# Linear attention: state updates dealt one sample at a time, and two loads of the small tokens' weights moved into the gate stage

## The chip, the cores and the metric

The kernel runs on one core of one Trainium2 chip. The metric is the device time of one launch in microseconds. The engines are named as in the profile: PE multiplies matrices, PEld loads its weights, DVE (VectorE), ACT (ScalarE) and POOL (GpSimd) work elementwise, and SP only issues DMAs. SPq is SP's queue: it issues in order, so a DMA that waits for a semaphore holds back those behind it.

## The reference, cut to what matters

One inference step of a two-layer trunk. A prompt of 1,024 tokens goes through gated linear attention (4 heads, key width 128, value width 256, 1024 channels), an MLP, differential attention and another MLP. Beside it go the **small tokens**: 16 meta tokens in front of the prompt and one new token of each of 8 running sequences, the samples. A sample's attention state (4 heads of 128 x 256) is read, used and written back updated:

```python
def gla_chunk(state, q, k, v, lg):
    ...
    o_inter = jnp.einsum('blhd,bhde->blhe', q * jnp.exp(b), state)
    ...
    new_state = jnp.exp(b_last)[..., None] * state + jnp.einsum(
        'blhd,blhe->bhde', k * jnp.exp(b_last[:, None] - b), v)
    return new_state, o_inter + o_intra
```

For a sample the chunk is a single token, so the new state is the old one scaled per key channel, plus the outer product of its key and its value. The small tokens then pass the rest of layer 0 (output projection, post-norm, MLP, post-norm) and the input projection of layer 1, all in the first sixth of the kernel.

## The kernel before, in words

The kernel is written in program order, and a planner lays down each engine's queue ahead of the run: it walks a modelled timeline, takes what is ready there, and the earlier line first where several are. So moving a line changes its rank among what the model holds ready, and not directly its place in the queue. On the chip each queue then runs in the order laid down, with semaphore waits.

All that the change touches lies in the first 500 us, the linear attention. Matmuls of the prompt are done in three passes of split operands (`mm3`, L206 to L208). The stages in program order are:

- Head 0's projections and decays; meanwhile the small tokens' input projection (L530, L539).
- The small tokens' own attention (L541 to L673). `state_in` (L638) loads a sample's state into one of five buffers: three in `Y`, columns 5120 to 8191, two in `st2`. L645 multiplies them with the queries into the bank `po`.
- `small_tokens` (L752) is a generator for the small tokens' way through the rest. A step is one pair of weight loads (`swt`, two buffers of 1 MB, loaded by `sload`, L234, or `sload2`, L240) and, at the next step, 16 matmuls of the pair (L685 or L696). There are 24 pairs: 2 of the attention's output weights, 8 and 8 of the MLP's, 4 and 2 of layer 1's input projection. Between them lie two post-norms (`s_post`, `s_ln`, L699 to L740: a copy out of the bank by DVE, four transposes, some fifteen small operations on DVE, and a logarithm and an exponential on ACT). The last step writes key and value rows and `sxd` to memory (L784 to L790).
- `state_updates` (L647): per sample a broadcast load of its value row into one of two halves of `Y`, columns 4096 to 6143 (L654), a multiply with the key by POOL (L655, 128x1024), four multiply-adds on DVE (L657, 128x256) and the store of the state (L658). Three samples' states are loaded a second time (L652). The second half of the value buffer overlaps the first state buffer, and the first half holds the samples' values `sv`, which L631 reads. In the kernel before all eight come in one go within step 3 of `small_tokens`, behind the first post-norm.
- Heads 1 to 3 (L798): eight groups of projections each (`proj`: four groups of query and key, four of value; `proj` yields after each, evictions L313, L315, L391), then for each half of the prompt `decays` (DVE and ACT, L435) and `advance` (L494), a serial chain.
- The gate stage (L812): for each head and half, 48 matmuls of the gate r, SiLU on ACT (L825), transposes, and L833 on DVE. Its results go into `Y`, which becomes the input of the output projection (`w_out`, L1001) after L997.

`deal` makes one step of `small_tokens`. In the kernel before it is called once ahead of head 1, then in each head behind groups 2, 4, 6 and 8 and behind both `decays`, and at the end of each half in the gate stage:

```python
for h in range(1, GH):
    for n, _ in enumerate(proj(h)):
        if n % 2:
            deal()
    ...
    for c in range(2):
        parts = decays(h, c, pgs[c])
        deal()
```

That makes 1 + 18 + 8 = 27 calls. The generator needs 25; the last two find it done. The second post-norm (call 19) falls to the second half of head 3, the last step (call 25) to the gate stage's third head.

Memory: buffers of the whole stage, `swt` among them, are given up at `p1.close()` (L836), behind the gate stage. The buffers of the paged attention, which starts there (L857 and on; pages by L877), are laid out after that.

Of the kernel before, what the change touches and what calls it, by code (L numbers as in the profile page):

```python
# [114 lines left out]
def hybrid_step(ctx, tc, A, dbg=None, upto=9):  # L115
# [4 lines left out]
    def bc(ap, shape, axis):  # L120
        return ap.unsqueeze(axis).broadcast_to(shape)
# [20 lines left out]
    def mmt():  # L142
        return banks["mm"].tile([P, 512], F32, name="mmt") if "mm" in banks else pairt()[:, 0]
# [4 lines left out]
    def smt():  # L148
        return banks["sm"].tile([P, 512], F32, name="smt")
# [48 lines left out]
    def kunit(w, c0):  # L198
        return unit(256, w.rearrange("(k p) n -> p k n", p=P)[:, :, c0 : c0 + 256])
# [5 lines left out]
    def mm3(ps, ah, al, bh, bl, first, last):  # L205
        TE.matmul(ps, ah, bh, start=first, stop=False)  # L206
        TE.matmul(ps, ah, bl, start=False, stop=False)  # L207
        return TE.matmul(ps, al, bh, start=False, stop=last)  # L208
# [13 lines left out]
    def s4():  # L222
        return spool.tile([P, 1024], F32, name="s4")

    def s2():
        return s2p.tile([P, 512], F32, name="s2")
# [33 lines left out]
    def qk_unit(h):  # L260
        return unit(P, *[wir[:, :, 512 * i + h * P : 512 * i + (h + 1) * P] for i in range(2)])
# [48 lines left out]
    def evict_qk(c, i, ps):  # L310
        t = g2.tile([P, 512], F32, name=("gq", "gk")[i])
        if i == 0:
            S.activation(t, ps, AF.Copy, scale=P ** -0.5)  # L313
        else:
            S.copy(t, ps)  # L315
        qk[c, i] = t
# [53 lines left out]
    def proj(h):  # L370
        hi, lo = qku if h == 0 else qk_unit(h)
        hv, lv = (w.rearrange("p (i k n) -> p i k n", i=2, n=P) for w in (hi, lo))
        for c in range(h == 0, 2):
            cs = slice(512 * c, 512 * c + 512)
            for i in range(2):
                ps = mmt()
                for k in range(NB):
                    mm3(ps, hv[:, i, k, :], lv[:, i, k, :], XH[:, k, cs], XL[:, k, cs], k == 0, k == NB - 1)
                evict_qk(c, i, ps)
                yield  # L380
        hi, lo = v0u if h == 0 else kunit(wi, 1024 + h * 256)
        hv, lv = (w.rearrange("p (k n) -> p k n", n=256) for w in (hi, lo))
        for c in range(2):
            for i2 in range(2):
                ps = mmt()
                for i in range(2):
                    t = 4 * c + 2 * i2 + i
                    for k in range(NB):
                        a = slice(t * P, (t + 1) * P)
                        mm3(ps[:, i * 256 : (i + 1) * 256], XH[:, k, a], XL[:, k, a], hv[:, k, :], lv[:, k, :], k == 0, k == NB - 1)  # L390
                S.copy(Yh[:, h, 4 * c + 2 * i2 : 4 * c + 2 * i2 + 2, :].rearrange("p i e -> p (i e)"), ps)  # L391
                yield
# [37 lines left out]
    def gate_in(h, c):  # L430
        pg = axt()
        TE.matmul(pg, wg[32 * c : 32 * c + 16, h * P : (h + 1) * P], gT[32 * c : 32 * c + 16, :], start=True, stop=True)
        return pg
# [159 lines left out]
    for hh in range(2):  # L593
        ps = smt()
        for i in range(2):
            h = 2 * hh + i
# [37 lines left out]
    def slot(i):  # L634
        t = Y[:, 5120 + 1024 * i : 6144 + 1024 * i] if i < 3 else st2[:, i - 3, :]
        return t.rearrange("p (h e) -> p h e", e=256)

    def state_in(b, i):  # L638
        with tc.issue_after(w_in):
            dma(slot(i), A["state_gla"][0, b].rearrange("h d e -> d h e"))  # L640
# [6 lines left out]
    def state_updates():  # L647

        for n, (b, i) in enumerate(((5, 0), (6, 1), (7, 2), (3, 3), (4, 4), (0, 3), (1, 4), (2, 3))):
            stt = slot(i)  # L650
            if b < 3:
                state_in(b, i)  # L652
            vb = Y[:, 4096 + 1024 * (n % 2) : 5120 + 1024 * (n % 2)].rearrange("p (h e) -> p h e", e=256)
            dma(vb.rearrange("p h e -> p (h e)"), A["vs"][b : b + 1, :].broadcast_to([P, D]))  # L654
            G.tensor_tensor(vb, vb, bc(skT[:, :, NM + b], [P, GH, 256], 2), op=ALU.mult)  # L655
            for h in range(GH):
                V.scalar_tensor_tensor(stt[:, h, :], stt[:, h, :], ses[:, h, b : b + 1], vb[:, h, :], ALU.mult, ALU.add)  # L657
            dma(A["gla_state_s"][0, b].rearrange("h d e -> d h e"), stt)  # L658

    so = spool.tile([P, 256], F32, name="so")  # L660
    ssq = spool.tile([P, 1], F32, name="ssq")
# [90 lines left out]
    def small_tokens():  # L752

        s_post((yield from s_rows(soT, A["gla_w_out"][0], NB)), 0, spool)
        state_updates()

        shT = s4().rearrange("p (k t) -> p k t", t=TS)
        for half in range(2):
            ps = yield from s_cols(sx, A["mlp_w1"][0], half * 2048)
            r = s2()  # L760
            S.activation(r, ps, AF.Relu)
            V.tensor_tensor(r, r, r, op=ALU.mult)
            pt = smt()
            for j in range(4):
                TE.transpose(pt[:, j * P : (j + 1) * P], r[:, j * P : (j + 1) * P], ident)
            V.tensor_copy(shT[:, 16 * half : 16 * half + 16, :].rearrange("p (c j) t -> p c j t", j=4),
                          pt.rearrange("p (j c t) -> p c j t", j=4, c=4))
        s_post((yield from s_rows(shT, A["mlp_w2"][0], 32)), 1, spool)

        pa = yield from s_cols(sx, wd, 0)  # L770
        sqkr = s2()
        S.copy(sqkr, pa)
        tmp = s2()[:, :128].rearrange("p (n d) -> p n d", d=16)
        rope(sqkr.rearrange("p (n d) -> p n d", d=64), pa.rearrange("p (n d) -> p n d", d=64), srope, 8, tmp)
        pb = yield from s_rows(sx, wd[:, 2048:3072], NB)
        svv = s2()
        S.copy(svv[64:, :], pb[64:, :])
        S.copy(svv[:64, :], svv[64:, :])
        V.tensor_tensor(svv[:64, :], svv[:64, :], pb[:64, :], op=ALU.add)
        for c in range(2):  # L780
            hs = slice(4 * c, 4 * c + 4)
            o = 64 + c * TS
            f = lambda ap: ap.rearrange("t h d -> t (h d)")
            dma(f(A["k_rows_p"][0, 0, 0:NM, hs, :]), sqkr[o : o + NM, :])  # L784
            dma(f(A["k_rows_s"][0, :, 0, hs, :]), sqkr[o + NM : o + NM + NS, :])
            dma(f(A["v_rows_p"][0, 0, 0:NM, hs, :]), svv[c * TS : c * TS + NM, :])
            dma(f(A["v_rows_s"][0, :, 0, hs, :]), svv[c * TS + NM : c * TS + NM + NS, :])
            dma(A["qs"][:, c * 512 : (c + 1) * 512], sqkr[c * TS + NM : c * TS + NM + NS, :])

        dma(A["sxd"], sx)  # L790

    small = small_tokens()

    def deal():
        next(small, None)

    deal()
    for h in range(1, GH):  # L798
        for n, _ in enumerate(proj(h)):
            if n % 2:  # L800
                deal()
        st = SM[:, h, :]
        pgs = [gate_in(h, c) for c in range(2)]
        for c in range(2):
            parts = decays(h, c, pgs[c])
            deal()
            st = advance(h, c, st, *parts)
        head_end(h, st)

# [2 lines left out]
    for h in range(GH):  # L812
        hi, lo = kunit(wi, 2048 + h * 256)
        hv, lv = (w.rearrange("p (k n) -> p k n", n=256) for w in (hi, lo))
        silt = st2.rearrange("p k (c n) -> p k c n", c=2)
        for c in range(2):
            cs = slice(512 * c, 512 * c + 512)
            sil, pts = [], []
            for m in range(2):
                ps = mmt()  # L820
                for k in range(NB):
                    ms = slice(m * P, (m + 1) * P)
                    mm3(ps, hv[:, k, ms], lv[:, k, ms], XH[:, k, cs], XL[:, k, cs], k == 0, k == NB - 1)
                s_ = silt[:, m, c, :]
                act = S.activation(s_, ps, AF.Silu).ins  # L825
                sil.append(s_)
                pt = axt()
                for i in range(4):
                    TE.transpose(pt[:, i * P : (i + 1) * P], Yh[:, h, 4 * c + i, m * P : (m + 1) * P], ident)
                pts.append(pt)  # L830
            deal()
            for m in range(2):
                V.scalar_tensor_tensor(fmv[:, h, c, m, :], pts[m], gn[:, m : m + 1], sil[m], ALU.mult, ALU.mult)  # L833
    with tc.issue_after(act):
        S.preload_act_table_set("natural_log_exp_and_others")
    p1.close()  # L836
# [548 lines left out]
    for step in steps + [None] * 0:  # L1385
        if step:
            h, n, t = step
# [356 lines left out]
```

## Time and profile before

| what | value |
|---|---|
| median of 3 runs | 2821.41 us (2813.26 to 2823.16) |
| the profiled execution | 2817.14 us |
| its span, first to last instruction | 2815.3 us |
| mean granted TensorE clock | 0.990 |
| PE busy | 2724.2 us (97%) |
| DVE, ACT, POOL busy | 1962.9, 1097.5, 1108.0 us |

The time of the profiled execution is 1.8 us over its span; what is shorter in the span is shorter in the time. PE is busy nearly throughout, so a change pays where PE stands idle or runs on a lower clock. Rows of the view by stretches give a stretch, its length, each engine's busy time with the number of its instructions, the granted clock, the DMA engines' busy share and the GB/s.

### The profile page before, as it was taken

How to read it: one execution, taken by the hardware profiler on the slowest of the kernel's cores; microseconds unless marked ns; L12 is line 12 of the kernel's file. 1: busy time of each engine (PE TensorE's matmuls, PEld its weight loads, DVE VectorE, ACT ScalarE, POOL GpSimd, SP SyncE). 2: the span in 40 equal slices, each digit the busy share in tenths (PEclk: the TensorE clock that was granted, in tenths of full speed). 3: DMA queues.
4: the chain of work that ended last, by engine and by line, in shares of the span. 5: the costliest groups of instructions: out<-in, count | busy, mean ns of one | idle time of the engine just before them, and what ended most of it. 6: DMA issues, size and time to landing. Idle time of an engine off the chain costs nothing.

```text
span 2815.3 us, 52242 instructions
## 1 busy us (share of the span) xinstructions
PE 2724.2 (97%) x19849; PEld 2238.2 (80%) x19849; DVE 1962.9 (70%) x3045; ACT 1097.5 (39%) x2232; POOL 1108.0 (39%) x744
## 2 busy tenths in 40 slices
PE   8988999999999999999999999899999999999997
PEld 5866766987777777777798989777898889798985
DVE  5365462578877787777568740887648888978788
ACT  4324363152221222222242112777525646355553
POOL 2142122334354343434233322200026767676774
PEclk9999999999999999999999999999999999999998
DMA  7565545735798898988658995212144555555684
GB/s 235 165 227 194 203 177 189 257 92 169 286 341 309 308 357 296 342 316 315 242 174 302 361 370 172 65 54 78 34 124 87 105 141 113 141 125 113 133 184 100
DMA packets 275624, 562.81 MB, mean 200 GB/s; under 512 B 23510, under 2 KB 144412, under 8 KB 271276
## 3 DMA queue, kind: packets, MB, share of 16 engines
q1 hardware_dynamic: 256076, 522.75, 53.9%
q0 software_dynamic: 19296, 36.71, 8.1%
q8 instruction: 156, 2.56, 0.4%
q14 instruction: 96, 0.79, 0.1%
HBM read 533.00 MB, written 29.52 MB: 200 GB/s over the span
## 4 chain that ended last, share of the span: by engine, by line
PE 78%; DVE 8%; DMA 5%; ACT 4%; issue 2%; POOL 2%; SPq 0%; DVEq 0%; POOLq 0%; ACTq 0%
PE mmt L206 18%; PE mmt L207 18%; PE mmt L208 18%; PE smt L949 4%; PE axt L206 3%; PE axt L207 3%; PE axt L208 3%; PE smt L1320 2%; ACT as L1298 1%; PE prt L1294 1%; DVE pg L908 1%; DMA swt<-in_mlp_w 1%; PE axt L1315 1%; POOL wlo L194 1%; DMA raw<-in_diff_w_in 1%
## 5 line engine op out<-in xcount | busy, mean ns | idle before, releaser
L194 POOL TENSOR_TENSOR wlo<-raw,whi 128x512 fp32r<-128x512 f32 x252 | 368.0, 1474 | 730.4 <-ACT whi L193 614.7
L206 PE MATMUL mmt<-whi,XH 128*128 128x256 f32 (+1 forms) x1760 | 524.3, 300 | 1.4 <-DVE ast L1296 0.9
L207 PE MATMUL mmt<-wlo,XH 128*128 128x256 f32 (+1 forms) x1760 | 522.1, 298 | 1.3 <-POOL wlo L194 1.3
L206 PE MATMUL mmt<-XH,whi 128*128 128x512 f32 (+1 forms) x1216 | 435.9, 360 | 7.1 <-DVE Y L1019 3.0
L208 PE MATMUL mmt<-XH,wlo 128*128 128x512 f32 (+1 forms) x1216 | 432.4, 356 | 0.0
L208 PE MATMUL mmt<-whi,XL 128*128 128x256 f32 x1536 | 431.7, 284 | 0.0
L193 ACT CAST whi<-raw 128x512 fp32r<-128x512 f32 x252 | 150.6, 619 | 572.9 <-DMA raw<-in_mlp_w 178.7
L206 PEld LDWEIGHTS mmt<-whi,XH 128*128 128x128 f32 x1760 | 330.4, 189 | 38.3 <-issue 25.1
L909 DVE TENSOR_REDUCE sc<-pg 128x16 f32<-128x1024 f32 x256 | 308.5, 1212 | 71.8 <-POOL pg L908 69.3
L207 PEld LDWEIGHTS mmt<-wlo,XH 128*128 128x128 f32 x1760 | 332.1, 189 | 18.5 <-issue 7.2
L207 PE MATMUL mmt<-XL,whi 128*128 128x512 f32 x768 | 306.9, 400 | 0.0
L908 DVE TENSOR_TENSOR pg<-pg,qb 128x1024 f32<-128x1024 f32 x192 | 258.9, 1355 | 66.6 <-DMA pg<-in_cache_k 49.7
L208 PEld LDWEIGHTS mmt<-whi,XL 128*128 128x128 f32 x1536 | 288.3, 189 | 4.8 <-issue 4.2
L206 PEld LDWEIGHTS mmt<-XH,whi 128*128 128x128 f32 x1216 | 229.8, 189 | 50.8 <-issue 7.9
L908 POOL TENSOR_TENSOR pg<-pg,qb 128x1024 f32<-128x1024 f32 x64 | 164.3, 2569 | 254.1 <-DMA pg<-in_cache_k 180.7
L208 PEld LDWEIGHTS mmt<-XH,wlo 128*128 128x128 f32 x1216 | 230.1, 189 | 36.3 <-issue 4.1
L206 PE MATMUL mmt<-whi,HH 128*128 128x512 f32 x512 | 205.3, 402 | 4.4 <-DVE Y L1133 4.4
L208 PE MATMUL mmt<-whi,HL 128*128 128x512 f32 x512 | 204.4, 399 | 0.0
L207 PE MATMUL mmt<-wlo,HH 128*128 128x512 f32 x512 | 203.9, 398 | 0.0
L1583 POOL TENSOR_TENSOR wlo<-RW,whi 128x512 fp32r<-128x512 f32 x96 | 167.0, 1771 | 66.3 <-ACT whi L1582 65.9
L1583 POOL TENSOR_TENSOR wlo<-rw,whi 128x512 fp32r<-128x512 f32 x92 | 155.6, 1768 | 78.3 <-ACT whi L1582 75.6
L207 PEld LDWEIGHTS mmt<-XL,whi 128*128 128x128 f32 x768 | 145.6, 190 | 37.4 <-issue 6.3
(438 smaller groups left out, 5729.2 us busy)
## 6 DMA issues: line engine op xcount, KB each, us to landing
pg<-in_cache_k SPq DMA_DIRECT2D x256, 512.0 KB
pg<-in_cache_v SPq DMA_DIRECT2D x256, 512.0 KB
raw<-in_mlp_w SPq DMA_DIRECT2D x164, 256.0 KB
swt<-in_mlp_w SPq DMA_DIRECT2D x32, 1024.0 KB
rw<-in_mlp_w SPq DMA_DIRECT2D x116, 256.0 KB
RW<-in_mlp_w POOLq DMA_DIRECT2D x96, 256.0 KB, 5.7
swt<-in_gla_w_in SPq DMA_DIRECT2D x12, 1024.0 KB
swt<-in_diff_w_in SPq DMA_DIRECT2D x12, 1024.0 KB
```

The costliest lines, as they stand in the source:

```text
L193: S.copy(hi[:, c], raw)
L194: G.tensor_tensor(lo[:, c], raw, hi[:, c].bitcast(F32), op=ALU.subtract)
L206: TE.matmul(ps, ah, bh, start=first, stop=False)
L207: TE.matmul(ps, ah, bl, start=False, stop=False)
L208: return TE.matmul(ps, al, bh, start=False, stop=last)
L908: eng.tensor_tensor(pg, pg, qb, op=ALU.mult)
L909: return V.tensor_reduce(sc[:, n, :], pg.rearrange("p (h d) -> p h d", d=64), op=ALU.add, axis=AX.X).ins
L949: m = TE.matmul(acc[i * TS : i * TS + 16, :256], w[r, n, :], pg[r, i * 256 : (i + 1) * 256], start=n == 0, stop=n == NPG).ins
L1294: TE.matmul(pss[m], qs[i][r, ts_], ks[j][r, x:y], start=i + j == 0, stop=i == 1)
L1298: S.activation(sc_[:, m, :W], sc_[:, m, :W], AF.Exp, bias=mns[:, m : m + 1], scale=-1.0, accum_out=l[:, m : m + 1])
L1320: TE.matmul(out, at, v, start=j == 0, stop=j == t + 1)
L1583: G.tensor_tensor(lo[:, k, :], t, hi[:, k, :].bitcast(F32), op=ALU.subtract)
```

## The change

- `state_updates` becomes a generator that yields after each sample. It is created beside `small_tokens`, and each of head 1's eight groups of projections is followed by one sample's update. So the updates no longer stand behind the first post-norm and ahead of the first pair of the MLP's weights; updates 1 to 3 come ahead of it, update 4 just ahead of its step, updates 5 to 8 behind it, between the next two pairs.
- In heads 2 and 3 the call of `deal` behind the first `decays` is dropped. That leaves 1 + 6 + 5 + 5 + 8 = 25 calls, so that two pairs more fall to the gate stage: the second post-norm goes to the gate stage's first head, second half, and the last step to its very end.
- Behind the gate stage a loop runs out what may be left of `small_tokens` (by this count nothing).

No arithmetic, load or store is added or dropped.

```diff
             dma(A["gla_state_s"][0, b].rearrange("h d e -> d h e"), stt)
+            yield
...
         s_post((yield from s_rows(soT, A["gla_w_out"][0], NB)), 0, spool)
-        state_updates()
-
...
-    small = small_tokens()
+    small, updates = small_tokens(), state_updates()
...
     deal()
     for h in range(1, GH):
         for n, _ in enumerate(proj(h)):
+            next(updates, None)
             if n % 2:
                 deal()
         st = SM[:, h, :]
         pgs = [gate_in(h, c) for c in range(2)]
         for c in range(2):
             parts = decays(h, c, pgs[c])
-            deal()
+            if c or h == 1:
+                deal()
             st = advance(h, c, st, *parts)
         head_end(h, st)
...
+    for _ in small:
+        pass
     with tc.issue_after(act):
         S.preload_act_table_set("natural_log_exp_and_others")
     p1.close()
```

## The prediction

> **What bounds the kernel now.** I read the page first: PE is the busiest engine by far.
>
> ```profile
> span 2815.3 us, 52242 instructions
> ...
> PE 2724.2 (97%) x19849; PEld 2238.2 (80%) x19849; DVE 1962.9 (70%) x3045; ACT 1097.5 (39%) x2232; POOL 1108.0 (39%) x744
> ```
>
> So 2815.3 - 2724.2 = 91.1 us is all that better order can win by filling PE's idle time. Next I read the view by stretches around the stages that the change touches, to see where those 91 us lie.
>
> ```profile
> 160.00:240.00 80.00, 65.33 (x632) 48.82 (x632) 60.96 (x113) 26.00 (x68) 33.69 (x16) 0.94 0.62 206
> ...
> 270.00:430.00 160.00, 151.57 (x1687) 108.88 (x1685) 92.18 (x198) 77.48 (x182) 31.97 (x19) 1.00 0.56 199
> 430.00:500.00 70.00, 69.88 (x382) 51.63 (x383) 22.73 (x40) 26.37 (x45) 18.04 (x12) 1.00 0.46 161
> ```
>
> PE idles 80.00 - 65.33 = 14.7 us between 160 and 240, where the updates run; 8.4 us in heads 2 and 3 (270 to 430); 0.1 us in the gate stage (430 to 500). The first stretch in steps of 10 us shows where, and that the clock falls twice:
>
> ```profile
> 180.00:190.00 10.00, 7.10 (x67) 4.52 (x59) 8.20 (x18) 5.05 (x15) 7.12 (x3) 1.00 1.02 344
> 190.00:200.00 10.00, 5.76 (x18) 4.73 (x19) 8.79 (x17) 1.45 (x4) 2.90 (x2) 0.66 0.86 293
> ...
> 210.00:220.00 10.00, 8.51 (x91) 7.65 (x89) 8.65 (x15) 4.36 (x9) 5.67 (x4) 1.00 0.42 134
> 220.00:230.00 10.00, 8.29 (x86) 5.68 (x85) 8.36 (x22) 4.61 (x16) 3.77 (x1) 1.00 0.44 128
> 230.00:240.00 10.00, 7.20 (x67) 4.18 (x68) 3.80 (x9) 3.63 (x13) 0.00 (x0) 0.84 0.52 197
> ```
>
> PE's waits in that stretch, then in the next:
>
> ```profile
> PE smt L707 <- DVE s L704: 7.1, 1, 7.1
> PE smt L696 <- DMA swt<-in_mlp_w: 2.8, 1, 2.8
> PE smt L696 <- DVE sx L740: 1.5, 1, 1.5
> PE axt L500 <- DVE At L475: 1.5, 1, 1.5
> ```
>
> ```profile
> PE smt L685 <- DMA swt<-in_mlp_w: 2.3, 2, 1.4
> ...
> PE axt L487 <- DVE t L483: 1.3, 1, 1.3
> PE axt L500 <- DVE At L475: 0.9, 1, 0.9
> PE smt L696 <- DVE sx L740: 0.5, 1, 0.5
> ```
>
> The longest one, 7.1 us, is the first post-norm's: its transposes (L707) wait for DVE's copy (L704). The chain of waits says what held DVE:
>
> ```profile
> 182.88 5.38 POOL Y L655
> ...
> 189.67 3.91 DVE st L657 x3
> 193.58 0.61 DVE s L704
> ...
> 194.24 1.12 PE smt L707 x4
> 195.35 0.43 PE mmt L207
> ...
> 198.76 0.43 PE mmt L206
> ...
> 199.46 0.23 PE mmt L208
> ```
>
> The copy stood behind an update's multiply-adds (L657) in DVE's queue, and these behind POOL's multiply (L655). After the stall nine matmuls from 195.35 to 198.76 took 0.43 us instead of 0.23.
>
> SP's queue tells the second story:
>
> ```profile
> 142.24 0.34 SPq L654 DMA_DIRECT2D Y<-vs  x1
> ...
> 193.61 13.10 SPq L658 DMA_DIRECT2D out_gla_state_s<-st  x2
> ...
> 218.16 0.38 SPq L658 DMA_DIRECT2D out_gla_state_s<-st  x1
> 218.64 8.95 SPq L191 DMA_DIRECT2D raw<-in_gla_w_in  x3
> 227.64 33.73 SPq L234 DMA_DIRECT2D swt<-in_mlp_w  x8
> ```
>
> The updates take SP from 142 to 218. Head 2's value weights (L191) and the second pair of the MLP's (L234, 227.64) are issued only then, and PE waits 2.8 us for that pair.
>
> **The change part by part.** Added instructions: none. Moved are eight updates, each one multiply on POOL, four multiply-adds on DVE and two or three DMAs on SP (value rows in, state out, for three a state in: 19), and 24 pairs of two DMAs each. Only their rank changes.
>
> *1. The post-norm's stall.* The program now ranks L704 ahead of updates 5 to 8. At stake are 7.1 us of idle PE and 9 x (0.43 - 0.23) = 1.8 us of slow matmuls: 8.9 us. But the planner's model puts L704 behind L657 only if it holds L657 ready earlier, and rank decides ties alone; between 0 and -8.9 I take two thirds, **-6.0**, being nearer to the row of the stall, since four updates are outranked and not one.
>
> The Trainium skill, "TensorE: Matmul & The Clock Gate", section "Why this matters for your kernels", says that a PE gap over about 3 us brings half clock. By that rule the 2.8 us wait would cost no clock and part 2 would be smaller by its clock term; the trace has 0.84 there, so I follow the trace.
>
> *2. SP's backlog.* The first pair of MLP weights now outranks updates 5 to 8, the second pair updates 7 and 8. PE's idle time from 210 to 240 is 1.49 + 1.71 + 2.80 = 6.0 us, plus 10 x (1 - 0.84) = 1.6 us of clock: 7.6. Only the 2.8 and its clock, and part of the post-norm's lateness (1.5), hang on the order of SP and DVE; the L500 wait is head 1's own chain. Between 0 and -7.6 I take **-2.5**. What comes later are updates 5 to 8: behind a waiting store stand the weights of head 2, and who waits last is head 2's value eviction, which overwrites the update's buffer:
>
> ```profile
> 169.96 0.59 ACT L391 COPY Y<-mmt 128x512 f32<-128x512 f32 x1 [7.17 <-PE mmt L208]
> ...
> 244.10 0.59 ACT L391 COPY Y<-mmt 128x512 f32<-128x512 f32 x1
> ```
>
> The last update's store is issued at 218.16, so 26 us cover a delay; with that gone, each microsecond of it is PE's, once its banks are full. The first row shows a limit: head 1's last value group was done at 169.96, while the updates' multiplies run to 211.5 (row in rival B). "Amid head 1's projections" is thus a rank; on the clock most updates run behind them, before and after.
>
> *3. Heads 2 and 3.* Two pairs leave (2 x 16 matmuls). PE's waits for `swt` (2.3), and the share of the second post-norm at head 3's end (1.3 + 0.9 + 0.5), are 5.0 us at most. Against it, PE waits there for DVE's chain too and loses fill, 2 x 1.92 = 3.8 us:
>
> ```profile
> 162.09 1.92 PE L685 MATMUL smt<-swt,soT 128*32 128x512 f32 x16
> ```
>
> Between +3.8 and -5.0 I take **-2.0**: gate matmuls can fill instead.
>
> *4. The gate stage.* It gets the two pairs and the post-norm. The matmuls cost nothing net (they left heads where PE was 95% busy). A logarithm and an exponential between SiLUs reload tables, as the logarithm does here:
>
> ```profile
> 417.10 1.28 ACT L731 ACT_TABLE_LOAD   x1
> ```
>
> Three loads (logarithm, exponential, SiLU), 3 x 1.28 = 3.9 us, lie under ACT's 70.00 - 26.37 us of slack and PE's three banks; if that cover is gone they cost 3.9. The end is more open: the last gate tile's eviction, the last pair's matmuls, and SP's queue.
>
> ```profile
> 497.10 0.59 ACT L825 ACTIVATE st<-mmt 128x512 f32<-128x512 f32 x1
> ```
>
> ```profile
> L685 PE MATMUL smt<-swt,sx x32: 592/592/617, 468.5 to 483.5; 128*32 128x512 f32 x32
> ```
>
> ```profile
> 486.57 0.34 SPq L786 DMA_DIRECT2D out_v_rows_p<-s  x1
> ...
> 500.56 5.73 SPq L1148 DMA_DIRECT2D Y<-in_x_prompt  x4
> 506.39 3.63 SPq L191 DMA_DIRECT2D raw<-in_gla_w_out  x2
> ```
>
> The last pair's matmuls now rank behind the last gate's, whose eviction was at 497.1; with 1.92 us of matmuls, and the 3.1 us from the last of them at 483.5 to the store of the value rows at 486.57, that store comes near 502, 16 us later. Behind it wait the prompt and the output weights. Cost 0 (if the pair is taken early, as PE may) to +16; I take **+1.5**, near the lower end, because the pairs so far were taken as they landed.
>
> *Sum*: -6.0 - 2.5 - 2.0 + 1.5 = **-9.0 us**. Against the profiled execution, 2817.1 - 9.0 = 2808.1. That one lies 4.3 us under the median of the runs, so the median to expect is 2821.4 - 9.0 = **2812 us**.
>
> **The rivals.** *A, all of it is won*: parts 1 to 3 at their ends, -8.9 - 7.6 - 5.0 = -21.5, so 2800. For it: the three rest on the same cause, the eight updates in one go. Against it: PE's waits for DVE's own decays are not touched.
>
> *B, the stall only moves*: an update's multiply on POOL meets DVE again and DVE's next copy waits behind it. The row for L655:
>
> ```profile
> L655 POOL TENSOR_TENSOR Y<-Y,sqk x8: 1902/1906/5365, 146.3 to 211.5; 128x1024 f32<-128x1024 f32 x8
> ```
>
> One of eight took 5.37 instead of 1.90, 3.5 us more. Then part 1 is nought, part 2 keeps -2.5, part 3 -2.0, part 4 +1.5, and one more such meeting adds about 2: -1, so 2820. Against it: seven of eight took near the least, and the change brings no DVE work earlier. This is also "the change doesn't do what it says". The Trainium skill, "SBUF — State Buffer", section "Who interferes with whom", has such a DVE operation and a reading POOL one exclude each other; the 5.37 agrees with it.
>
> *C, slower, by the end of the gate stage*: the last step is late, the value rows' store holds SP's queue, and the prompt and output weights come up to 16 us late. It decides from 10.5 us on, where it eats parts 1 to 3: -10.5 + 16 = +5.5, so 2827. For it: only 0.1 us of PE's time is idle in the gate stage, so nothing there hides it. Against it: between the store at 486.57 and the prompt's loads at 500.56 lie 14 us in which a later store finds room, and the pairs may come earlier than ranked if the first post-norm does.
>
> **How the numbers follow.** Forecast (2812) 0.40, A 0.27, B 0.18, C 0.15. The range 2795 to 2830 holds B, C and A down to 5 us under its number; the likeliest's own is 2805 to 2818. About 0.5%, 14 us, is what a measurement of this kernel can tell from no change: 2807.3 and 2835.5. Faster: 0.85 of A, 0.28 of the forecast and a little of B, 0.35. Slower: a third of C, and a tenth of B and a twentieth of the forecast for shifts later in the kernel that no row names, 0.09. The rest, 0.56, within.
>
> **What would show it.** Part 1: no wait of L707 over 2 us, and the clock at 1.00 from 190 to 200. Part 2: the second pair of MLP weights issued before 215, PE over 73 us busy of 160 to 240. Part 3: no `swt` wait in heads 2 and 3. Part 4: PE still full in the last 70 us of the stage, the first w_out weights and prompt rows no later than 506 less the gain. It is wrong if a wait on L655 or L657 holds PE again, if head 2's eviction waits for an update, or if the output weights of 506.39 come more than 8 us later.

## The result, and the profile after

The changed kernel takes 2809.96 us (median of 15 runs, 2801.72 to 2815.93), the kernel before 2818.75 us in the same comparison (15 runs): a ratio of 0.9971, 95% interval 0.9961 to 0.9981, or 8.8 us less. The profiled execution took 2804.0 us, 6 us under that median, so that the two profiles lie further apart (13 us) than the kernels do.

The page of the changed kernel:

```profile
span 2802.2 us, 52241 instructions
...
PE 2715.8 (97%) x19849; PEld 2233.8 (80%) x19849; DVE 1954.0 (70%) x3045; ACT 1096.4 (39%) x2233; POOL 1105.1 (39%) x744
```

PE's idle time is 2802.2 - 2715.8 = 86.4 us, against 91.1. The view by stretches of the changed kernel, with the columns that the prediction's rows have:

```profile
160.00:240.00 80.00, 66.49 (x779) 51.17 (x778) 62.94 (x121) 28.19 (x74) 31.94 (x16) 0.98 0.64 218
...
190.00:200.00 10.00, 7.08 (x88) 5.73 (x88) 7.92 (x18) 1.66 (x5) 1.98 (x1) 0.83 0.77 268
...
270.00:430.00 160.00, 154.40 (x1697) 111.95 (x1687) 90.73 (x197) 79.87 (x185) 34.45 (x19) 1.00 0.59 207
430.00:500.00 70.00, 70.00 (x397) 54.20 (x396) 24.16 (x44) 23.79 (x41) 14.07 (x11) 1.00 0.52 171
```

In head 1 (160 to 240), where the forecast put most of the gain, PE is busy 1.2 us longer; in heads 2 and 3 (270 to 430) 2.8 us. The 1.2 us can't be the change's: on PE, DVE, ACT, POOL and SP alike, the two traces have the same order of instructions up to 372.39 us of the kernel before, which lies in head 3. PE's waits in the changed kernel, first from 150 to 260, then from 270 to 430 (line numbers past 658 differ from the kernel before's by one to three):

```profile
PE smt L708 <- DVE s L705: 5.7, 1, 5.7
PE smt L697 <- DMA swt<-in_mlp_w: 2.7, 1, 2.7
```

```profile
PE axt L467 <- DVE t L424: 2.0, 2, 1.6
PE smt L686 <- DMA swt<-in_mlp_w: 1.8, 2, 1.1
...
PE smt L697 <- DVE sx L741: 0.5, 1, 0.5
```

The first post-norm's stall is still there (L708, 5.7 us instead of 7.1), so are the 2.7 us for the second pair of MLP weights. In heads 2 and 3 the two waits for DVE's decays are gone (L487 1.3 and L500 0.9 before).

By the program's count two pairs and the second post-norm move to the gate stage. On the chip they don't. Five pairs come behind head 3's last state in each kernel (from 431.2 to 482.1 us before, from 423.5 to 487.1 after), and the second post-norm's copy stays 29 us ahead of that state (428.9 before, 421.3 after):

```profile
400.06 0.69 DVE L704 COPY s<-smt 128x512 f32<-128x512 f32 x1 [1.35 <-PE smt L685]
```

```profile
392.70 0.69 DVE L705 COPY s<-smt 128x512 f32<-128x512 f32 x1 [1.83 <-PE smt L686]
```

What the change does to the order begins in head 3's first decays. The timeline before, PE's and DVE's rows alone, the projections' and the gate's matmuls left out:

```profile
370.53 0.44 PE L452 MATMUL axt<-t 128*32 128x32 f32 x26
...
372.39 1.92 PE L685 MATMUL smt<-swt,s 128*32 128x512 f32 x16 [1.43 <-DMA swt<-in_mlp_w]
...
374.13 0.55 PE L452 MATMUL axt<-t 128*32 128x32 f32 x38
374.46 0.70 DVE L461 COPY_PREDICATED gAd<-masks,axt 128x128 f32<-128x128 uint8 x2 [4.19 <-PE axt L452]
```

and after:

```profile
366.62 0.76 PE L452 MATMUL axt<-t 128*32 128x32 f32 x64
367.15 0.70 DVE L461 COPY_PREDICATED gAd<-masks,axt 128x128 f32<-128x128 uint8 x2 [0.78 <-PE axt L452]
...
368.51 1.92 PE L686 MATMUL smt<-swt,s 128*32 128x512 f32 x16 [1.13 <-DMA swt<-in_mlp_w]
```

Before, a pair of MLP weights stood in PE's queue in the middle of the decays' block matmuls (L452, 26 before it and 38 behind it). PE waited 1.43 us for the weights, and DVE's L461, which needs the rest of those blocks, waited 4.19 us. After, all 64 go first, DVE waits 0.78 us, and PE waits for the weights only then. Head 3's length, from the last eviction of its values (L391) to its last state (L504), before and after:

```profile
L391 ACT COPY Y<-mmt x16: 566/586/590, 71.7 to 352.2; 128x512 f32<-128x512 f32 x16
L504 DVE SCALAR_TENSOR_TENSOR gS<-gS,geb,axt x28: 467/480/484, 132.8 to 428.9; 128x256 f32<-128x256 f32 x28
```

```profile
L391 ACT COPY Y<-mmt x16: 562/585/587, 71.8 to 348.3; 128x512 f32<-128x512 f32 x16
L504 DVE SCALAR_TENSOR_TENSOR gS<-gS,geb,axt x28: 467/481/482, 132.9 to 421.3; 128x256 f32<-128x256 f32 x28
```

428.9 - 352.2 = 76.7 us before, 421.3 - 348.3 = 73.0 us after: 3.7 us. DVE's shorter wait isn't yet that gain, since in head 3 PE waited for no L461 in either kernel. PE's own time in these stretches is the measure, before and after:

```profile
352.20:428.90 76.70, 71.84 (x770) 49.96 (x771) 46.59 (x104) 45.46 (x95) 13.91 (x9) 1.00 0.51 183
```

```profile
348.30:421.30 73.00, 70.93 (x770) 49.87 (x771) 44.59 (x104) 46.69 (x96) 13.80 (x9) 1.00 0.54 193
```

For the same number of matmuls PE is idle 76.70 - 71.84 = 4.9 us before and 73.00 - 70.93 = 2.1 after, 2.8 us less, and busy 0.9 us less. The idle time goes at the head's end. PE's rows there, before and after:

```profile
416.19 0.48 PE L208 MATMUL mmt<-XH,wlo 128*128 128x512 f32 x1
417.95 0.63 PE L487 MATMUL axt<-c_ident,t 128*128 128x128 f32 x4 [1.29 <-DVE t L483]
419.45 0.67 PE L500 MATMUL axt<-Y,At 128*128 128x256 f32 x2 [0.86 <-DVE At L475]
```

```profile
408.88 0.47 PE L207 MATMUL mmt<-XL,whi 128*128 128x512 f32 x1
...
411.30 0.39 PE L208 MATMUL mmt<-XH,wlo 128*128 128x512 f32 x1
411.53 0.60 PE L487 MATMUL axt<-c_ident,t 128*128 128x128 f32 x4
411.97 0.60 PE L500 MATMUL axt<-Y,At 128*128 128x256 f32 x2
```

Behind the last block matmuls one gate matmul is left before, eleven after (from 408.88 to 411.30, one every 0.23 us), and PE no longer waits. The ten stood between the first two runs of blocks before (from 376.35 us). So head 3's gain is mostly this: gate matmuls saved up for the end fill PE's waits there. The ten and the pair changed places together in every kernel run, so that no run shows what either is worth alone, and what shortens the busy time isn't shown.

SP's queue after:

```profile
225.60 11.25 SPq L234 DMA_DIRECT2D swt<-in_mlp_w  x4
...
491.12 3.38 SPq L1151 DMA_DIRECT2D Y<-in_x_prompt  x3
495.19 2.27 SPq L785 DMA_DIRECT2D out_v_rows_p<-s  x1
...
498.24 0.32 SPq L786 DMA_DIRECT2D out_v_rows_s<-s  x1
498.60 0.40 SPq L1151 DMA_DIRECT2D Y<-in_x_prompt  x1
499.09 2.46 SPq L191 DMA_DIRECT2D raw<-in_gla_w_out  x2
```

The last of the value rows' stores is issued at 498.24 instead of 487.69, 10.5 us later, but three of the four prompt loads went ahead of them, and the two loads of output weights that stood at 506.39 come 7.3 us earlier (499.09).

### The profile page after: what moved, and what is told of

The parts are those of the page before. It is cut to its first block, busy times and chain, and to the rows that moved or that the text cites. A ratio compares the mean times of both kernels' runs of the same rounds, so it can differ in the third digit from the quotient of the medians.

```text
span 2802.2 us, 52241 instructions
## 1 busy us (share of the span) xinstructions
PE 2715.8 (97%) x19849; PEld 2233.8 (80%) x19849; DVE 1954.0 (70%) x3045; ACT 1096.4 (39%) x2233; POOL 1105.1 (39%) x744
## 4 chain that ended last, share of the span: by engine, by line
PE 74%; DVE 8%; ACT 4%; DMA 3%; issue 2%; POOL 1%; SPq 0%; DVEq 0%; POOLq 0%; ACTq 0%
PE mmt L206 17%; PE mmt L207 17%; PE mmt L208 17%; PE smt L952 4%; PE axt L206 3%; PE axt L207 3%; PE axt L208 3%; PE smt L1323 2%; ACT as L1301 2%; DVE pg L911 1%; PE prt L1297 1%; DMA swt<-in_mlp_w 1%; PE axt L1318 1%; DMA rw<-in_mlp_w 1%; PE smt L686 1%
## 5 line engine op out<-in xcount | busy, mean ns | idle before, releaser
L194 POOL TENSOR_TENSOR wlo<-raw,whi 128x512 fp32r<-128x512 f32 x252 | 364.4, 1459 | 730.6 <-ACT whi L193 599.6
L912 DVE TENSOR_REDUCE sc<-pg 128x16 f32<-128x1024 f32 x256 | 308.2, 1211 | 70.5 <-POOL pg L911 68.1
```

What stands on the lines that cost most here:

```text
L194: G.tensor_tensor(lo[:, c], raw, hi[:, c].bitcast(F32), op=ALU.subtract)
L912: return V.tensor_reduce(sc[:, n, :], pg.rearrange("p (h d) -> p h d", d=64), op=ALU.add, axis=AX.X).ins
```

## The experiments

The same lengths were read from the profile of each kernel run; they are differences of such first and last rows. "Head 1 to 3" is from the first state (the first L504 row, `gS<-SM`) to head 3's last value eviction; "gate, w_out" is from there on to the last eviction of the first w_out; "MLP" is to the last addition of the first MLP. All in us, one execution each; the ratio is that of the medians' comparison with the kernel before on the same chip. The first nine kernels run the same order up to head 3's first decays, so that their "head 1 to 3", 219.4 to 224.8 us, shows how far single executions differ, and not the change.

| kernel | head 1 to 3 | head 3 | gate, w_out | MLP | ratio, 95% interval |
|---|---|---|---|---|---|
| before | 223.3 | 76.7 | 162.6 | 833.0 | 1 |
| updates_only | 224.5 | 76.9 | 162.1 | 835.4 | 1.0006 [0.9993, 1.0018] |
| after | 219.4 | 73.0 | 161.5 | 831.1 | 0.9971 [0.9961, 0.9981] |
| after_again | 222.3 | 73.1 | 162.3 | 830.1 | 0.9977 [0.9964, 0.9990] |
| deals_only | 222.4 | 73.0 | 161.5 | 830.4 | 0.9990 [0.9976, 1.0004] |
| drop_h2 | 224.2 | 73.6 | 162.7 | 835.8 | 0.9992 [0.9976, 1.0007] |
| drop_h3 | 224.8 | 77.7 | 162.9 | 832.8 | 1.0014 [0.9999, 1.0029] |
| head_only | 220.4 | 73.0 | 162.1 | 835.9 | 0.9988 [0.9974, 1.0002] |
| gate_late | 223.5 | 76.7 | 161.4 | 831.3 | 0.9994 [0.9981, 1.0008] |
| copy_first | 218.7 | 80.7 | 164.4 | 831.0 | 1.0003 [0.9991, 1.0015] |
| copy_act | 218.1 | 77.8 | 163.2 | 833.0 | 0.9981 [0.9966, 0.9996] |
| copy_act0 | 221.0 | 77.6 | 162.8 | 832.9 | 0.9992 [0.9980, 1.0003] |
| copy_act0_late | 219.4 | 77.7 | 163.5 | 830.6 | 0.9988 [0.9975, 1.0001] |
| drop_four | 222.3 | 76.6 | 169.2 | 837.9 | 1.0056 [1.0042, 1.0070] |

**Which half of the change acts.** The updates one by one, with the calls of `deal` as before (the edit is to the changed kernel, as in all that follow but the deals alone):

```diff
         for c in range(2):
             parts = decays(h, c, pgs[c])
-            if c or h == 1:
-                deal()
+            deal()
```

> The updates dealt one by one amid head 1's projections, the calls of deal as in the kernel before (27). The queues of all five engines hold the same instructions in the same order as the kernel before. Theory 1 (the updates' new rank does nothing, all of the gain is the two dropped calls): 0 against before, within 2 us; the post-norm's stall stays between 5 and 8 us. The prediction's parts 1 and 2 (the updates' rank frees the post-norm and SP): 8 us faster.

1.0006, and an interval around 1: no gain. The trace tells why more sharply than the time: on each of the five engines this kernel's instructions stand in the same order as in the kernel before, from first to last. The updates have another place in the source and another rank, and the planner sets them down where it did. So the forecast's parts 1 and 2 had no cause. The other half alone (`state_updates` in one go as before, the two calls left out, the loop over `small` behind the gate stage), and the changed kernel once more:

> The kernel before with the other half of the change alone: two calls of deal fewer (second and third head's first decays) and the loop that uses up the rest behind the gate stage, the states' updates in one go as before. If the gain is made by the later pairs of weights alone, this is the changed kernel: ratio 0.9960 to 0.9982, head 3 from the v projection's last eviction to its end 73.0 us (before 76.7), gate stage 66.4 us (before 68.2). If the updates' place matters when the pairs are also dealt later, it stays above 0.9985. A second question is the first post-norm's stall in head 1: if it is shorter (5.7 us) in the changed kernel because of the changed order, it is so here; if it varies from one execution to the next, it may be 7.1 us as in the kernel before.

> The changed kernel once more, nothing else. Its first measurement was 0.9971 [0.9961, 0.9981] of the kernel before; the deals alone, whose engines run the same instructions in the same order, 0.9990 [0.9976, 1.0004]. If these are the same program and the difference is that of the chips and rounds, this run lies between the two, 0.9970 to 0.9990. If the updates' place in the source does something that the order of the instructions doesn't show, it comes out at 0.9961 to 0.9978 again. The first post-norm's stall of head 1 shows whether 5.7 us belonged to the changed kernel or to one execution: 7 us or more here would say the latter.

The deals alone give the same order as the changed kernel on every engine. The three runs of this order gave 0.9971, 0.9977 and 0.9990, whose intervals share 0.9976 to 0.9981; their mean is 0.9979, 5.8 us. The first number was the lucky one of the three.

They also settle whose the stall's 5.7 us was. PE's wait in head 1, the stretch from 160 to 240, and from the timeline the multiply on POOL (L655) and DVE's multiply-adds (L657) that meet ahead of the post-norm's copy, in the deals alone:

```profile
PE smt L707 <- DVE s L704: 7.7, 1, 7.7
...
160.00:240.00 80.00, 65.48 (x725) 48.81 (x724) 61.02 (x116) 27.61 (x73) 32.00 (x16) 0.94 0.65 214
...
180.52 5.96 POOL L655 TENSOR_TENSOR Y<-Y,sqk 128x1024 f32<-128x1024 f32 x1 [3.49 <-DMA Y<-vs]
...
186.51 5.31 DVE L657 SCALAR_TENSOR_TENSOR st<-st,ses,Y 128x256 f32<-128x256 f32 x4 [1.79 <-POOL Y L655]
```

and in the changed kernel's second profile:

```profile
PE axt L467 <- DVE t L424: 3.9, 1, 3.9
...
PE smt L708 <- DVE s L705: 2.6, 1, 2.6
...
160.00:240.00 80.00, 66.60 (x727) 49.85 (x727) 59.85 (x115) 27.88 (x73) 31.51 (x16) 0.91 0.65 214
...
180.39 5.35 DVE L657 SCALAR_TENSOR_TENSOR st<-st,ses,Y 128x256 f32<-128x256 f32 x4
...
180.63 2.01 POOL L655 TENSOR_TENSOR Y<-Y,sqk 128x1024 f32<-128x1024 f32 x1 [3.31 <-DVE t L418]
```

With the same order of instructions the stall was 7.7 us in one execution and 2.6 in another. In the first the multiply on POOL took 5.96 us while DVE was at work, and DVE's next multiply-adds waited for it; in the second it took 2.01 us, and the multiply-adds that had begun just ahead of it took 5.35 instead of 1.67. And the 5.1 us between the stalls bought only 66.60 - 65.48 = 1.1 us of busy PE, since in the second PE had waited 3.9 us for DVE just ahead of the post-norm (L467). The Trainium skill, "SBUF — State Buffer", section "Who interferes with whom", has such pairs of operations exclude each other; the rows agree, and show beside it that the length differs between executions.

**Which call.** Only one of the two calls left out, head 2's or head 3's:

```diff
-            if c or h == 1:
+            if c or h != 2:      # drop_h2; drop_h3 has h != 3
                 deal()
```

> The changed kernel with the call behind the first decays dropped in head 2 alone (26 calls, one pair more in the gate stage). Up to the gate stage its queues are the changed kernel's. Theory 2 (the gain is in head 3, where a pair of the MLP's second weights now ranks behind the decays' small matmuls, so that the second half's decays start earlier): 4 to 7 us faster than before, head 3's last state 3 to 4 us earlier than in the kernel before relative to the end of head 2. Rival (each dropped call gives the same, by fewer loads in heads 2 and 3): 4.4 us. Rival (the gain is in the end of the gate stage, from both): under 3 us.

> The call dropped in head 3 alone (26 calls). Up to the middle of the gate stage its queues are those of the kernel before, and only the last pair and what follows differ. Theory 2: head 3 as in the kernel before, so 0 to 3 us faster. Rival (each dropped call gives the same): 4.4 us.

Head 2's call alone brings head 3's gain (73.6 us); head 3's alone doesn't (77.7). The call left out in head 2 moves no instruction of head 2: up to the gate stage the order is the changed kernel's, which differs from before only from the pair at 372.39 us on. The one left out in head 3 moves nothing ahead of 468.5 us, in the gate stage. So where a call is left out and where the order changes lie far apart, and how the planner comes from one to the other isn't shown. Of the time nothing is shown either: the ratios, 0.9992 and 1.0014, can't be told from 1, and the 4 to 7 us that theory 2 gave head 2's call didn't come.

**Head 3 or the gate stage.** Two kernels part them. In the first the heads are those of the changed kernel and the gate stage's first place makes up the two calls; in the second the heads are as before and the gate stage's first two calls are left out:

```diff
 # head_only, from the changed kernel, in the gate stage
-            deal()
+            for _ in range(1 if h or c else 3):
+                deal()
 # gate_late, from the changed kernel
-            if c or h == 1:
-                deal()
+            deal()
...
-            deal()
+            if h:
+                deal()
```

> The changed kernel's head 3 with the kernel before's gate stage: both calls of deal are left out of heads 2 and 3, and the gate stage's first place calls deal three times instead of once, so that steps 18 and 19 of the small tokens fall at the gate stage's start and steps 20 to 25 where the kernel before has them. Theory H (the gain is made in head 3, where the block matmuls of the first decays go ahead of a wait for MLP weights, and the gate stage only passes it on): head 3's end from the v projection's last eviction takes 73 to 74 us (before 76.7, after 73.0), and the ratio is 0.9985 to 0.9990, with most of what is left of the 8.8 us unexplained by it. Theory G (the gain is made by where the gate stage's steps lie): head 3 as in H, but the gate stage gives it back; 0.9995 to 1.0005. Theory W (both are needed, since the first drop by itself did nothing): as G in number, with the loss at the start of the gate stage, where three calls lie together.

> The other half: the heads' calls of deal as in the kernel before, and the gate stage's first two calls left out, so that head 3 is as before and steps 20 to 25 of the small tokens fall into the gate stage where the changed kernel has them (last at head 3's second half). Theory H (head 3): head 3 takes 76.7 us as before and the ratio is 0.9995 to 1.0005. Theory G (the gate stage's steps): the gate stage takes 66.4 us instead of 68.2, the start of the first MLP 1 to 2 us less, and the ratio is 0.9975 to 0.9985. Theory C, the late end of the gate stage (the small tokens' value rows 10 us later, amid the loads that follow): 1.0000 to 1.0030.

The view by stretches from 340 to 440 has one row for each kernel. Before:

```profile
340.00:440.00 100.00, 94.34 (x927) 67.12 (x922) 52.43 (x115) 51.57 (x111) 21.95 (x12) 1.00 0.53 190
```

after:

```profile
340.00:440.00 100.00, 97.13 (x935) 69.87 (x934) 51.90 (x117) 55.22 (x115) 26.42 (x16) 1.00 0.51 183
```

head_only:

```profile
340.00:440.00 100.00, 97.23 (x933) 68.26 (x932) 51.42 (x116) 54.52 (x112) 26.98 (x16) 1.00 0.53 192
```

gate_late:

```profile
340.00:440.00 100.00, 94.37 (x918) 67.13 (x917) 53.90 (x117) 52.67 (x112) 24.22 (x14) 1.00 0.50 181
```

Head 3's gain goes with the heads' calls alone (97.2 against 94.4 of 100 us; 73.0 against 76.7). PE's waits of 1.3 and 0.9 us (L487, L500) at its end stand in all four kernels with 76.7 to 77.7 us (before, updates_only, drop_h3, gate_late) and in none of the five with 73.0 to 73.6. The rest seems to go with the gate stage's calls: in the table, the four kernels with the late steps (after, after_again, deals_only, gate_late) have 830 to 831 us of first MLP, those with the gate stage as before (before, updates_only, drop_h2, drop_h3, head_only) 833 to 836. Part of it is PE's wait at that MLP's start, which in the kernel before reads

```profile
PE mmt L206 <- DVE Y L1133: 2.3, 1, 2.3
```

and is 1.7, 1.5, 1.4 and 2.2 us in updates_only, head_only, drop_h2 and drop_h3, but none, 0.5, none and 0.4 us in the four. With PE's waits there for the splits of operands (L203 on DVE, L194 on POOL) it comes to 3.7 to 5.3 us in the five and 2.1 to 2.7 in the four, about 2 us. Late steps alone don't secure it: copy_act and copy_act0, further down, have them too, and waits of 3.8 and 3.5 us and MLPs of 833 us. By the medians' ratios the halves are worth 0.9988 and 0.9994, together 0.9982, near the 0.9979 of the changed kernel's three runs. But either one's interval holds 1. So theory H (head 3) is shown by head 3's length, and not by the time; theory G has the 2 us at the MLP's start, from single executions, and its ratio for gate_late (0.9975 to 0.9985) didn't come. The gate stage alone is 66.3 us long in the four, as G said, and 68.1 to 68.3 in the five, but w_out then takes 95.1 to 96.0 us instead of 94.0 to 94.5. Theory C's loss from the late end of the gate stage isn't there: gate_late has it, with value rows at 502, and loses nothing.

**What the first post-norm's stall is worth.** Since the change doesn't touch it, four kernels take it away by other means, each from the changed kernel:

```diff
 # copy_first: updates 5 to 7 behind the post-norm's copy
-            V.tensor_copy(sev, ps)
+            held.append(V.tensor_copy(sev, ps).ins)
...
-            for h in range(GH):
+            with tc.issue_after(held[0]) if n > 4 else nullcontext():
+              for h in range(GH):
 # copy_act: both copies on ScalarE
-            V.tensor_copy(sev, ps)
+            S.copy(sev, ps)
 # copy_act0: the first one only
-            V.tensor_copy(sev, ps)
+            (V.tensor_copy if ln else S.copy)(sev, ps)
 # copy_act0_late: copy_act0, and
-            if n % 2:
+            if n % 2 and (h, n) != (3, 1):
                 deal()
...
-            deal()
+            for _ in range(1 if h or c else 2):
+                deal()
```

> The changed kernel with one thing more: of the states' updates 5 to 7 VectorE's part is held back behind the first post-norm's copy of its PSUM, so that the copy no longer stands behind an update that waits for GpSimd. This is what the forecast's part 1 took the change to do. If that stall is worth its length, the wait of the first post-norm's transposes for the copy (5.7 us in the changed kernel, 7.1 before) goes, TensorE is busy over 70 of the 80 us from 160 to 240, and the time is 4 to 6 us below the changed kernel's: ratio 0.9950 to 0.9960 against the kernel before. If the stall's end is set by what is queued next (the updates themselves, head 1's scans behind them, GpSimd), it only moves: 0.9965 to 0.9980, as the changed kernel.

> The changed kernel with the first two post-norms' copies of their PSUM made by ScalarE instead of VectorE: the copy stands behind nothing that waits for GpSimd. If part 1's stall is worth its length, as for the other edit: the transposes' wait of 5.7 us goes to under 2 us and the ratio is 0.9950 to 0.9960. If VectorE's backlog holds the next step instead (the sums of the post-norm, L717 and on, stand behind the same updates): the wait shifts to the mean's matmul, and the ratio is 0.9965 to 0.9980.

> The changed kernel with only the first post-norm's copy made by ScalarE; the second's stays on VectorE. With both copies on ScalarE, TensorE was busy 71.3 of the 80 us from 160 to 240 (changed kernel 66.5), but head 3 took 77.8 us instead of 73.0, so that the ratio was 0.9981. If head 3's loss came from the second copy on ScalarE: head 3 at 73 to 74 us, ratio 0.9945 to 0.9965. If it came from the planner's other order of head 3, which follows from an earlier end of head 1: head 3 at 77 to 78 us again, ratio 0.9970 to 0.9985.

> The same with head 3's first call of deal left out and made up by two calls at the gate stage's first place: the pairs of MLP weights come one place later in head 3, as if head 1 had not been shortened. If head 3's time hangs on where the pairs' matmuls fall among the first decays' block matmuls: head 3 at 73 to 75 us with head 1's gain kept, ratio 0.9945 to 0.9965, below the changed kernel. If head 3 is bound otherwise: 77 us and 0.9975 to 0.9990.

With both copies on ScalarE, PE's first wait of 160 to 240 and the stretches:

```profile
PE smt L722 <- DVE ss L720: 5.3, 1, 5.3
...
160.00:240.00 80.00, 71.32 (x828) 54.91 (x821) 60.69 (x127) 30.67 (x78) 30.34 (x15) 0.94 0.75 256
340.00:440.00 100.00, 92.74 (x892) 66.91 (x891) 52.08 (x115) 52.45 (x110) 24.59 (x15) 0.98 0.49 175
```

The copy's wait is gone and its like appears one step on: the mean's matmul (L722) waits 5.3 us for DVE's sums, which stand behind the same updates. Still, PE is busy 4.8 us more in this stretch, and by head 3 some of that is kept (218.1 us against 219.4 to 222.4 in the three runs of the changed kernel's order). Then head 3 takes 77.8 us instead of 73.0. All four kernels gained in head 1 (PE 68.5 to 71.3 us of the 80) and lost in head 3 (77.6 to 80.7), and none came out below the changed kernel's three runs (0.9971 to 0.9990). Dealing one pair later in head 3, as if head 1 were not shortened, didn't mend that (77.7), nor did leaving the second copy on VectorE (77.6). So the stall isn't worth its length: what is taken away there appears in part one step on and, by the lengths, the rest is lost in head 3. That the planner's other order of head 3 is to blame fits all four, but no run shows it, and copy_first's 1.0003 and copy_act0's 0.9992 lie outside what either theory said. No order with both gains was found.

**How late the end may come.** Four calls fewer instead of two (heads 2 and 3 without the ones in their decays):

```diff
-            if c or h == 1:
+            if h == 1:
                 deal()
```

> Both calls behind the decays dropped in heads 2 and 3 (23 calls: 1 + 6 + 4 + 4 + 8), so the last two steps of the small tokens come behind the gate stage, in the closing loop. Rival C of the prediction (the late end holds SP's queue and the first output weights): slower than the changed kernel by 5 to 16 us, the value rows stored after 505. Theory 2 with small tokens taken as they land, whatever their rank: within 4 us of the changed kernel.

Here the last steps come behind the gate stage. Its value rows and the stretches behind it:

```profile
527.54 0.31 SPq L786 DMA_DIRECT2D out_v_rows_s<-s  x1
...
500.00:600.00 100.00, 96.56 (x780) 92.05 (x780) 62.09 (x90) 23.05 (x34) 29.22 (x23) 0.98 0.66 226
600.00:700.00 100.00, 93.79 (x415) 75.18 (x414) 77.72 (x82) 32.46 (x56) 36.92 (x22) 0.98 0.43 137
```

The changed kernel's PE is busy 100.00 and 97.90 us in these two. The gate stage and w_out take 169.2 us instead of 161.5, the MLP 837.9, and the ratio is 1.0056, some 22 us above the changed kernel's three runs where 5 to 16 were expected. DVE's first addition of w_out (L1024) waits 9.6 us for the prompt's rows, and PE 3.4 us for that addition. So the loss that rival C names is real, two calls beyond the change.

## Why the prediction was right, and where not

The number was right: 2812 forecast, 2810.0 measured; -9.0 us against -8.8, or -5.8 as the mean of the three runs of this order; and it is within 0.5% of before, the outcome given the largest chance. Its sum was right by luck: of the 8.5 us that it took from parts 1 and 2 nothing came, and what parts 3 and 4 cover gained more than they said.

**Part 1** (-6.0) fell. Its step was "the program now ranks L704 ahead of updates 5 to 8". The rank did change; the order didn't. The condition that the part itself put on it (the planner puts the copy behind L657 only if it holds L657 ready earlier, and rank decides ties alone) was the whole answer, and 0, the end of the range that this gives, should have been the value. Its marks failed: the wait was 5.7 us where under 2 was said, the clock 0.83 where 1.00 was. And 8.9 us was too much for the stall even where it is taken away: copy_act has 4.8 us more of busy PE, 1.3 to 4.3 us by head 3.

**Part 2** (-2.5) fell with it. The second pair of MLP weights is issued at 225.60 where "before 215" was said, and PE is busy 66.49 us where "over 73" was; the wait for that pair is 2.7 us, as before.

**Part 3** (-2.0, from +3.8 to -5.0) had sign and range right, with -3.7 us in head 3, the same in head_only and in all runs of this order. Its ground was in the main wrong. "Two pairs leave" was read from the program; no pair left heads 2 and 3. The waits of 1.3 and 0.9 us at head 3's end weren't the post-norm's share, for they are gone while the post-norm, with its own wait of 0.5 us, is still there. The mark "no `swt` wait in heads 2 and 3" failed: 1.8 of 2.3 us remain. What did come true is its last half sentence, "gate matmuls can fill instead": ten of them, moved within head 3, fill those two waits.

**Part 4** (+1.5, 0 to +16) foresaw that the end comes later, though not by its step (the stage got no two pairs and no post-norm; its last four pairs lie further apart), and had the sign wrong. The value rows came 10.5 us later, but SP had issued three prompt loads ahead of them; gate stage and w_out took 161.4 to 162.3 us instead of 162.6, and the MLP behind 2 to 3 us less. The marks on this part held: PE is full from 430 to 500, and the weights of 506.39 come earlier by 7.3 us. They aren't "the first w_out weights", though; the first of those were issued at 446.79 in the kernel before.

**The rivals.** B's claim that the change doesn't do what it says is true of the updates, word for word, and its mechanism (the stall only moves) showed itself in after_again, where 5.1 us less of one wait bought 1.1. The -2.5 it left to part 2 didn't come. The gain it left to parts 3 and 4 (-0.5) was too small. A fell with parts 1 and 2. C decides later than it said: 10.5 us of lateness cost nothing, some 40 us (drop_four) cost 0.56%.

## What to carry to other kernels

Before pricing a change of rank or of place in the source, ask whether any engine's order of instructions changes at all; where a planner orders by readiness, it may not. Then price a stage by the busiest engine's own time. DVE's wait of 4.19 us in head 3 was the most striking row, but PE waited for no result of that step; what the stage gained is 2.8 us of PE's idle time, most of it two waits that ten matmuls now fill (in the kernel before they ran earlier), and 0.9 us of its busy time. Matmuls that nobody needs yet are worth most where the busiest engine would otherwise stand idle. And a stall taken away upstream shifts all that is ordered downstream: judge it by the end of the last stage it touches, not by the stretch where it was.

## What was not expected of the hardware

The same order of instructions gives stalls of quite different length: the 128x1024 multiply on POOL ahead of the first post-norm took 2.01, 3.67 and 5.96 us in three profiles of one order (1.90 is the usual), and the post-norm's stall 2.6 (with a wait of 3.9 just ahead of it), 5.7 and 7.7 us. A difference of a few microseconds between two single profiles is therefore no evidence of a cause in a kernel like this; head 3's 73.0, 73.1, 73.0 and 73.0 us against 76.7, 76.9 and 76.7 are.
